# Tracing a four-layer attention network as one block, ordered by a finer engine model

## The chip, the cores and the metric

The kernel runs on one core of one Trainium2 chip. The core has five engines that matter here: PE (TensorE, the matrix engine), DVE (VectorE), ACT (ScalarE), POOL (GpSimd) and SP (SyncE, which issues the transfers). Each engine works through its own list of instructions in the order in which the build has put them, and waits on semaphores where it needs what another engine makes. The metric is the time of one execution on the device in microseconds; of several runs the median is taken.

## The reference

The reference is a network of two parts over 256 latent rows and 256 context rows of width 1024, in float32. The first part has four layers with the same frame and different mixers: attention with grouped heads and a window (layer 0), latent attention with low-rank queries and keys (layer 1), a matrix LSTM in chunks (layer 2), and grouped attention again (layer 3).

```python
layers = [window_gqa_mixer, mla_mixer, mlstm_mixer, window_gqa_mixer]   # shortened
for i in range(4):
    sh_l, sc_l, gt_l = modulation(c, w_ada, b_ada)
    sh_c, sc_c, gt_c = modulation(c_ctx, w_ada, b_ada)
    h_l = rmsnorm(x_lat, g_pre) * (1.0 + sc_l[:, None, :]) + sh_l[:, None, :]
    h_c = rmsnorm(x_ctx, g_pre) * (1.0 + sc_c) + sh_c
    y_l, y_c = mixer(h_l, h_c, need_ctx=i < 3)
    x_lat = x_lat + gt_l[:, None, :] * rmsnorm(y_l, g_post)
    if i < 3: x_ctx = x_ctx + gt_c * rmsnorm(y_c, g_post)
```

The second part works on the latent rows alone: one projection, three mixers side by side (a sparse one, one with a window, one with forget gates), a gated merge of the three, an output projection, and a feed-forward part with a convolution.

```python
h = rms_norm(x, norm_mix); cols = split_columns(h @ w_in)
o_a, o_b, o_c = nsa_mixer(cols, ...), swa_mixer(cols, ...), fox_mixer(cols, ...)
proj = einsum('btnm,nmd->btnd', stack([o_a, o_b, o_c]), w_branch)
x = x + (sigmoid(cols['merge']) * proj).sum(axis=2) @ w_out
x = x + conv_ffn(rms_norm(x, norm_ffn), w_gate, w_up, conv_w, conv_b, w_down)
```

## The kernel before

Every product of two float32 matrices is made of three matmuls on rounded halves: a value is split into a high half and the rest, and high by high, low by high and high by low are summed in one PSUM bank. In `gemm_a` these are L366, L367 and L368 (512 columns each), in `gemm_b` L378, L379 and L381 (256 columns). Weights come from DRAM in pieces of 512 KB: `load_part` has SP load a piece (L356), ACT copy its high half (L345, into wh or Q) and DVE subtract for the low one (L347, into wl or P). PSUM tiles come from three sets of banks: three named mm for products, two named S for scores, three named tp for transposes and small sums.

The two streams, c (context) and l (latent), lie in xc0, xc1, xl0 and xl1 of 128 rows each. `normed` squares them on ACT (L603) for the sum of squares and scales them on DVE (L606). `turn` transposes the result on PE (L618, four transposes into one tp bank), modulates it on ACT (L625, two for each bank) and splits it on DVE (L627 and L628, into thc and tlc or thl and tll). With that the first products of a layer can start.

At the end of a layer, `out_proj` makes four products of 24 matmuls for each stream, one for each half of the width and each 128 rows. Behind each one ACT squares the bank (L663) and DVE multiplies it by a gate (L664), after which the bank is free. `finish` does the `turn` of the stream that was finished before; it is called within `out_proj` of the other stream (L661), at the product whose number is in the constant FIN.

Attention in layers 0 and 3 (`gqa`) takes a head at a time: two matmuls and a mask make a score tile S (L908, L909, L912), DVE takes the row maxima (L913, L914), ACT the exponentials (L921), DVE scales by the row sums (L929, four for a group of four heads), PE transposes (L942), ACT and DVE copy the transposes out in turn (L736, L740), and PE multiplies them by the values (L947). Layer 1 (`mla`) has the same steps as `softmax` (L1110 to L1129) and `back` (L1142 to L1155), layer 2 (`mlstm`) its own. A filler, `ada_steps`, issues the modulation of the next layer a piece at a time (L540, eight small matmuls together) at a pace set by the table PACE.

The text of the kernel sets dependencies, not the order on the engines. All instructions are traced first. When the context closes, the framework puts those of each engine in order, with a model of how long each one takes; program order and a few marked priorities decide between those that are ready. The last lines of the kernel, where the change is, open the net's context and run it: `Net.run` first does the setup and the first `turn`, then the four layers, then the mixers and the feed-forward part.

Of the kernel before, what the change touches and what calls it, by code (L numbers as in the profile page):

```python
# [2036 lines left out]


def body(tc, A, out, upto=99):
    with ExitStack() as stack:  # L2040
        net = Net(tc, A, out, stack, upto)
        with net.inner_guard():
            net.run()
# [18 lines left out]
```

## Time and profile before

| | us |
|---|---|
| median of three runs | 1456.51 (1456.22 to 1456.57) |
| the profiled execution's own time | 1455.3 |
| its span | 1453.5 |
| PE busy | 1418.6 |
| DVE busy | 1044.2 |
| ACT busy | 736.0 |
| POOL busy | 51.5 |

The profile shows one execution. Its page gives the busy time of each engine, then the chain of work that ended last, followed back from the last instruction; the views behind it list what an engine waited for, the busy time of a stretch, and single instructions in order of time. A matmul's shown length is longer than the distance to the next one, since matmuls are pipelined: the distance between two starts is what it costs the engine. The granted clock of the execution is 0.998 of full speed in the mean.

### The profile page before, as it was taken

The numbers are of one execution on the slowest core, as the hardware profiler recorded it, in microseconds if no ns is written. First come the engines' busy times: TensorE is split into PE (matmuls) and PEld (weight loads), VectorE is DVE, ScalarE is ACT, GpSimd is POOL, SyncE is SP. The second block draws the span as 40 slices with busy tenths as digits, with TensorE's granted clock in tenths as the row PEclk, the third lists the DMA queues.
The fourth block names the chain that finished last, engine by engine and source line by source line (L and its number), as shares of the span: only waits on it lengthen the run. The fifth ranks groups of instructions, "written<-read, shape, count | busy, mean of one in ns | idle before, by whom it ended". The sixth has DMA issues, their size and how long they took to land.

```text
span 1453.5 us, 24554 instructions
## 1 busy us (share of the span) xinstructions
PE 1418.6 (98%) x9445; PEld 1172.7 (81%) x9445; DVE 1044.2 (72%) x2241; ACT 736.0 (51%) x1447; POOL 51.5 (4%) x72
## 2 busy tenths in 40 slices
PE   7999999999999999999999999999999999999998
PEld 4776778789787778887778776778878888799987
DVE  4587866653788667793765867889687877799863
ACT  3455544442556344552634544556576555465542
POOL 0000000000000000010100000000000000211200
PEclk9999999999999999999999999999999999999999
DMA  9541215345602214515252532157524534455552
GB/s 379 202 163 44 74 56 207 94 149 186 208 32 62 73 48 147 201 52 173 87 198 73 173 125 65 60 180 240 159 96 138 174 117 158 164 198 184 180 182 97
DMA packets 63555, 203.35 MB, mean 140 GB/s; under 512 B 10329, under 2 KB 14542, under 8 KB 63438
## 3 DMA queue, kind: packets, MB, share of 16 engines
q1 hardware_dynamic: 63438, 201.79, 41.2%
q8 instruction: 74, 1.21, 0.3%
q14 instruction: 43, 0.35, 0.1%
HBM read 200.65 MB, written 1.11 MB: 139 GB/s over the span
## 4 chain that ended last, share of the span: by engine, by line
PE 82%; DVE 8%; ACT 4%; issue 3%; DMA 2%; POOL 0%; SPq 0%; ACTq 0%; DVEq 0%; POOLq 0%
PE mm L366 10%; PE mm L368 10%; PE mm L367 10%; PE mm L378 8%; PE mm L381 8%; PE mm L379 8%; PE tp L947 3%; PE tp L942 3%; PE tp L540 2%; PE tp L744 2%; PE S L378 1%; PE S L379 1%; PE S L381 1%; PE S L908 1%; DVE wl L347 1%
## 5 line engine op out<-in xcount | busy, mean ns | idle before, releaser
L347 DVE TENSOR_TENSOR wl<-wr,wh 128x1024 fp32r<-128x1024 f32 (+5 forms) x168 | 196.8, 1182 | 70.8 <-ACT wh L345 68.8
L345 ACT ACTIVATE wh<-wr 128x1024 fp32r<-128x1024 f32 (+5 forms) x172 | 174.5, 1027 | 96.6 <-PE mm L379 28.0
L378 PE MATMUL mm<-thl,wh 128*128 128x256 f32 x608 | 175.6, 289 | 0.0
L381 PE MATMUL mm<-thl,wl 128*128 128x256 f32 x608 | 174.0, 287 | 0.7 <-DVE wl L347 0.7
L379 PE MATMUL mm<-tll,wh 128*128 128x256 f32 x608 | 174.2, 287 | 0.0
L366 PE MATMUL mm<-wh,thl 128*128 128x512 f32 (+3 forms) x312 | 123.2, 395 | 0.8 <-ACT thl L693 0.5
L368 PE MATMUL mm<-wh,tll 128*128 128x512 f32 (+3 forms) x312 | 122.4, 393 | 0.0
L367 PE MATMUL mm<-wl,thl 128*128 128x512 f32 (+3 forms) x312 | 122.0, 391 | 0.0
L378 PEld LDWEIGHTS mm<-thl,wh 128*128 128x128 f32 x608 | 116.3, 191 | 4.0 <-issue 3.2
L381 PEld LDWEIGHTS mm<-thl,wl 128*128 128x128 f32 x608 | 116.0, 191 | 3.0 <-issue 1.5
L379 PEld LDWEIGHTS mm<-tll,wh 128*128 128x128 f32 x608 | 116.5, 192 | 1.5 <-issue 1.2
L366 PE MATMUL mm<-wh,thc 128*128 128x512 f32 (+2 forms) x232 | 91.5, 395 | 2.1 <-DVE thc L627 1.6
L368 PE MATMUL mm<-wh,tlc 128*128 128x512 f32 (+2 forms) x240 | 92.6, 388 | 0.5 <-DVE tlc L1918 0.3
L367 PE MATMUL mm<-wl,thc 128*128 128x512 f32 (+2 forms) x232 | 90.9, 393 | 0.0
L347 DVE TENSOR_TENSOR wl<-wrd,wh 128x1024 fp32r<-128x1024 f32 x52 | 65.9, 1270 | 26.8 <-ACT wh L345 26.5
L921 ACT ACTIVATE P<-S,nm 128x512 f32<-128x512 f32 (+1 forms) x96 | 58.5, 613 | 44.6 <-DVE nm L914 40.9
L366 PEld LDWEIGHTS mm<-wh,thl 128*128 128x128 f32 x312 | 58.7, 188 | 12.5 <-issue 1.6
L368 PEld LDWEIGHTS mm<-wh,tll 128*128 128x128 f32 x312 | 58.7, 188 | 10.8 <-issue 0.6
L345 ACT ACTIVATE wh<-wrd 128x1024 fp32r<-128x1024 f32 x52 | 53.5, 1050 | 26.0 <-PE mm L367 23.0
L367 PEld LDWEIGHTS mm<-wl,thl 128*128 128x128 f32 x312 | 58.8, 188 | 9.4
L378 PE MATMUL mm<-thc,wh 128*128 128x256 f32 (+1 forms) x216 | 65.3, 302 | 0.6 <-DVE thl L752 0.6
L381 PE MATMUL mm<-thc,wl 128*128 128x256 f32 (+1 forms) x216 | 63.4, 293 | 0.0
(564 smaller groups left out, 3730.6 us busy)
## 6 DMA issues: line engine op xcount, KB each, us to landing
ar<-in_w_l_ada_dram SPq DMA_DIRECT2D x80, 512.0 KB
wr<-in_w_l_in_dram SPq DMA_DIRECT2D x48, 512.0 KB
wr<-in_w_l_out_dram SPq DMA_DIRECT2D x32, 512.0 KB
wr<-in_w_s_mg_dram SPq DMA_DIRECT2D x24, 512.0 KB
wrd<-in_w_s_down_dram SPq DMA_DIRECT2D x22, 512.0 KB
wrd<-in_w_s_gate_dram SPq DMA_DIRECT2D x20, 512.0 KB
wrd<-in_w_s_up_dram SPq DMA_DIRECT2D x20, 512.0 KB
wr<-in_w_s_br_dram SPq DMA_DIRECT2D x12, 512.0 KB
```

What stands on the lines that cost most here:

```text
L345: nc.scalar.activation(hi[:, :kc * n], raw[:, :kc * n], AF.Copy)
L347: eng.tensor_sub(lo[:, :kc * n], raw[:, :kc * n], hi[:, :kc * n].bitcast(F32))
L366: nc.tensor.matmul(ps, xh(kk), wh[:, k, n0:n0 + n], start=kk == 0, stop=False)
L367: nc.tensor.matmul(ps, xh(kk), wl[:, k, n0:n0 + n], start=False, stop=False)
L368: nc.tensor.matmul(ps, xl(kk), wh[:, k, n0:n0 + n], start=False, stop=kk == KC - 1)
L378: nc.tensor.matmul(ps, wh[:, k, n0:n0 + m], xh(kk), start=kk == 0, stop=False)
L379: nc.tensor.matmul(ps, wh[:, k, n0:n0 + m], xl(kk), start=False, stop=False)
L381: nc.tensor.matmul(ps, wl[:, k, n0:n0 + m], xh(kk), start=False, stop=kk == KC - 1)
L540: return self.nc.tensor.matmul(ps[32 * g:32 * g + 32, :], self.cs[:, k, :], r[:, g * 256:(g + 1) * 256], start=k0 == 0 and i == 0, stop=k0 ...
L921: nc.scalar.activation(p[:, :nk], ps[:, i, :], AF.Exp, scale=scale, bias=nm[:, r:r + 1], accum_out=sm[:, r:r + 1])
L942: nc.tensor.transpose(tp[:, r, :], P[r][:, j * 128:(j + 1) * 128], self.eye)
L947: nc.tensor.matmul(o[i * 64:(i + 1) * 64, kv], vv, pT[:, 2 * i:2 * i + 2, :], start=j == 0, stop=j == nj - 1)
```

## The change

`body` opens a named block around everything that it traces. The block's instructions are put in order when it closes, and its argument asks for the finer of the framework's two timing models of the engines for that. Nothing that is computed changes, nor does any tile, number of slots or constant.

```diff
 def body(tc, A, out, upto=99):
-    with ExitStack() as stack:
+    with tc.block(name="all", schedule_with_timeline_sim=True), ExitStack() as stack:
         net = Net(tc, A, out, stack, upto)
         with net.inner_guard():
             net.run()
```

Both kernels have the same instructions on each engine: 8723 matmuls and transposes on PE, 2145 on DVE, 1177 on ACT, 68 on POOL and 469 transfers on SP. Of these, 6387 on PE, 1701 on DVE, 883 on ACT, 3 on POOL and 219 on SP stand at another place in their engine's row. (The page counts more on PE, since some matmuls leave two records.) The row of the feed-forward part is nearly the same. In the rows below a name such as mm1013_5584 is a tile and the number of its buffer; the same buffer has a number higher by one in the changed kernel.

The first place is the start, on ACT: xn13 and xn14 are the squares of the context stream, Q434 and Q435 those of the latent one, and mid29 is the first modulated tile. Before:

```order
L603 ACTIVATE xn13_107,ss12_106<-xc0_75 128x1024
L446 ACTIVATE th0_89<-cc_81 128x16
L603 ACTIVATE xn14_108,ss12_106<-xc1_76 128x1024
L497 ACTIVATE mid24_168<-tp19_126 128x128
L345 ACTIVATE wh31_192<-wr30_190 128x1024
L625 ACTIVATE mid29_185<-tp28_180,bclc7_100,acolc5_98 128x256 x2
L603 ACTIVATE Q434_199,ss33_198<-xl0_77 128x1024
L603 ACTIVATE Q435_200,ss33_198<-xl1_78 128x1024
L625 ACTIVATE mid41_223<-tp40_218,bcll6_99,acoll4_97 128x256 x2
```

Now:

```order
L603 ACTIVATE xn13_108,ss12_107<-xc0_76 128x1024
L603 ACTIVATE xn14_109,ss12_107<-xc1_77 128x1024
L446 ACTIVATE th0_90<-cc_82 128x16
L497 ACTIVATE mid24_169<-tp19_127 128x128
L345 ACTIVATE wh31_193<-wr30_191 128x1024
L603 ACTIVATE Q434_200,ss33_199<-xl0_78 128x1024
L625 ACTIVATE mid29_186<-tp28_181,bclc7_101,acolc5_99 128x256 x2
L603 ACTIVATE Q435_201,ss33_199<-xl1_79 128x1024
L345 ACTIVATE wh54_294<-wr53_292 128x1024
```

The square of xl0 (Q434) moved ahead of the L625 of mid29, and the square of xc1 ahead of the small tanh (L446).

The second place is the hand-over from layer 1 to layer 2, first on PE. mm1013 and mm1014 are the last two products of the latent stream's output, tp1004 to tp1010 the transposes of the context stream. Before:

```order
L618 MATMUL tp1008_5535<-eye_83,xn993_5467 128x128
L618 MATMUL tp1008_5535<-eye_83,xn992_5466 128x128
L618 MATMUL tp1008_5535<-eye_83,xn993_5467 128x128
L366 MATMUL mm1013_5584<-Q4968_5315,thl952_5276 128x512
L367 MATMUL mm1013_5584<-P4969_5316,thl952_5276 128x512
L618 MATMUL tp1010_5545<-eye_83,xn992_5466 128x128
L618 MATMUL tp1010_5545<-eye_83,xn993_5467 128x128
L618 MATMUL tp1010_5545<-eye_83,xn992_5466 128x128
L618 MATMUL tp1010_5545<-eye_83,xn993_5467 128x128
L368 MATMUL mm1013_5584<-Q4968_5315,tll953_5277 128x512
```

Now:

```order
L618 MATMUL tp1008_5536<-eye_84,xn993_5468 128x128
L618 MATMUL tp1008_5536<-eye_84,xn992_5467 128x128
L618 MATMUL tp1008_5536<-eye_84,xn993_5468 128x128
L618 MATMUL tp1010_5546<-eye_84,xn992_5467 128x128
L618 MATMUL tp1010_5546<-eye_84,xn993_5468 128x128
L618 MATMUL tp1010_5546<-eye_84,xn992_5467 128x128
L618 MATMUL tp1010_5546<-eye_84,xn993_5468 128x128
L366 MATMUL mm1014_5612<-Q4968_5316,thl952_5277 128x512
L367 MATMUL mm1014_5612<-P4969_5317,thl952_5277 128x512
L368 MATMUL mm1014_5612<-Q4968_5316,tll953_5278 128x512
```

The 24 matmuls of mm1013 now stand in one piece ahead of the 16 transposes, and mm1014 right behind these; before, 19 matmuls of mm1013 stood behind the last transpose. On ACT at the same place, where mid1005 to mid1011 are the modulated tiles and mm1001 and mm1012 the two products ahead of mm1013, before:

```order
L625 ACTIVATE mid1005_5520<-tp1004_5515,bclc585_3187,acolc583_3185 128x256 x2
L625 ACTIVATE mid1007_5530<-tp1006_5525,bclc585_3187,acolc583_3185 128x256 x2
L625 ACTIVATE mid1009_5540<-tp1008_5535,bclc585_3187,acolc583_3185 128x256 x2
L625 ACTIVATE mid1011_5550<-tp1010_5545,bclc585_3187,acolc583_3185 128x256 x2
L663 ACTIVATE yg998_5485,ss1000_5487<-mm1001_5488 128x512
L663 ACTIVATE yg999_5486,ss1000_5487<-mm1012_5557 128x512
```

Now:

```order
L625 ACTIVATE mid1005_5521<-tp1004_5516,bclc585_3188,acolc583_3186 128x256 x2
L625 ACTIVATE mid1007_5531<-tp1006_5526,bclc585_3188,acolc583_3186 128x256 x2
L625 ACTIVATE mid1009_5541<-tp1008_5536,bclc585_3188,acolc583_3186 128x256 x2
L663 ACTIVATE yg998_5486,ss1000_5488<-mm1001_5489 128x512
L625 ACTIVATE mid1011_5551<-tp1010_5546,bclc585_3188,acolc583_3186 128x256 x2
L663 ACTIVATE yg999_5487,ss1000_5488<-mm1012_5558 128x512
```

The first L663 moved ahead of the last pair of L625 and still stands behind six L625. mm1480, mm1481 and mm1468 stand in the same way at the hand-over from layer 2 to layer 3.

The third place is the last heads of layer 3, on PE, where mm1778 is a projection of that layer and S1680, S1682, S1695 and S1697 are scores. Before:

```order
L912 MATMUL S1680_9355<-mask_469,eyeb_474 128x128
L381 MATMUL mm1778_9869<-thl1469_8351,wl1769_9802 128x256
L908 MATMUL S1682_9363<-K81498_8521,Q41662_9263 128x512
L909 MATMUL S1682_9363<-K81499_8522,Q41662_9263 128x512
L912 LDWEIGHTS eyeb_474
L912 MATMUL S1682_9363<-mask_469,eyeb_474 128x128
L378 MATMUL mm1778_9869<-thl1469_8351,wh1771_9807 128x256
L379 MATMUL mm1778_9869<-tll1470_8352,wh1771_9807 128x256
L908 MATMUL S1695_9418<-K81498_8521,Q41662_9263 128x512
L909 MATMUL S1695_9418<-K81499_8522,Q41662_9263 128x512
L912 LDWEIGHTS eyeb_474
L912 MATMUL S1695_9418<-mask_469,eyeb_474 128x128
```

Now:

```order
L912 MATMUL S1680_9356<-mask_470,eyeb_475 128x128
L908 MATMUL S1682_9364<-K81498_8522,Q41662_9264 128x512
L909 MATMUL S1682_9364<-K81499_8523,Q41662_9264 128x512
L912 LDWEIGHTS eyeb_475
L912 MATMUL S1682_9364<-mask_470,eyeb_475 128x128
L908 MATMUL S1695_9419<-K81498_8522,Q41662_9264 128x512
L909 MATMUL S1695_9419<-K81499_8523,Q41662_9264 128x512
L912 LDWEIGHTS eyeb_475
L912 MATMUL S1695_9419<-mask_470,eyeb_475 128x128
L908 MATMUL S1697_9427<-K81498_8522,Q41662_9264 128x512
L909 MATMUL S1697_9427<-K81499_8523,Q41662_9264 128x512
```

The matmuls of the projection left the spaces between the scores, where three stood within these rows and twelve between S1697 and the first transpose behind it; they stand ahead of scores of earlier heads.

## Rows read from the trace of the kernel before

**Rows 1.** The page: busy time of PE, chain by engine, the costliest DVE group

```profile
PE 1418.6 (98%) x9445; PEld 1172.7 (81%) x9445; DVE 1044.2 (72%) x2241; ACT 736.0 (51%) x1447; POOL 51.5 (4%) x72
...
PE 82%; DVE 8%; ACT 4%; issue 3%; DMA 2%; POOL 0%; SPq 0%; ACTq 0%; DVEq 0%; POOLq 0%
...
L347 DVE TENSOR_TENSOR wl<-wr,wh 128x1024 fp32r<-128x1024 f32 (+5 forms) x168 | 196.8, 1182 | 70.8 <-ACT wh L345 68.8
```

**Rows 2.** PE's waits: us in total, number of times, longest one

```profile
PE tp L494 <- DMA P<-in_w_l_mod_dram: 7.6, 2, 7.4
PE tp L744 <- DVE xl L1928: 3.1, 2, 2.0
...
PE tp L618 <- DVE xn L606: 2.3, 4, 1.3
...
PE S L908 <- ACT P L921: 1.4, 1, 1.4
PE tp L744 <- DVE P L1361: 1.3, 3, 0.7
PE S L1110 <- ACT P L1125: 1.2, 1, 1.2
PE tp L1150 <- ACT T L1145: 1.2, 2, 0.7
```

**Rows 3.** Busy time by stretch: us, PE, PEld, DVE, ACT, POOL, granted clock, DMA

```profile
24.00:278.00 254.00, 253.47 (x1842) 193.45 (x1843) 174.66 (x404) 122.50 (x270) 0.00 (x0) 1.00 0.38 134
388.00:482.00 94.00, 89.94 (x548) 73.75 (x547) 81.69 (x198) 57.64 (x133) 0.00 (x0) 1.00 0.25 84
910.00:950.00 40.00, 37.59 (x248) 26.66 (x247) 32.70 (x78) 23.72 (x54) 0.00 (x0) 1.00 0.18 61
1245.00:1262.00 17.00, 13.92 (x72) 11.41 (x71) 14.35 (x16) 9.16 (x12) 9.98 (x4) 0.96 0.37 125
```

**Rows 4.** In order of time, 14 to 18 us, ACT and PE: start, length, idle before

```profile
15.08 1.05 ACT L603 ACTIVATE Q<-xl 128x1024 f32<-128x1024 f32 x1
...
15.71 0.79 PE L366 MATMUL mm<-wh,thc 128*128 128x512 f32 x1 [1.57 <-DVE thc L627]
```

**Rows 5.** In order of time, 508 to 517 us, the hand-over to layer 2

```profile
508.35 0.40 PE L366 MATMUL mm<-Q,thl 128*128 128x512 f32 x1
...
510.50 3.75 ACT L625 ACTIVATE mid<-tp,bclc,acolc 128x256 f32<-128x256 f32 x8 [1.17 <-PE tp L618]
...
512.30 0.39 PE L366 MATMUL mm<-Q,thl 128*128 128x512 f32 x1
...
514.10 0.63 ACT L663 ACTIVATE yg<-mm 128x512 f32<-128x512 f32 x1
...
515.08 0.69 DVE L664 TENSOR_TENSOR yg<-mm,K 128x512 f32<-128x512 f32 x1
...
516.49 0.39 PE L366 MATMUL mm<-Q,thl 128*128 128x512 f32 x1
```

**Rows 6.** In order of time, 915 to 927 us, softmax and values in layer 3

```profile
915.48 0.23 PE L912 MATMUL S<-mask,eyeb 128*128 128x128 bf16 x1
...
915.75 1.42 DVE L913 TENSOR_REDUCE mx<-S 128x1 f32<-128x512 f32 x2
...
917.33 0.69 ACT L921 ACTIVATE P<-S,nm 128x512 f32<-128x512 f32 x1 [0.83 <-DVE nm L914]
...
918.16 0.50 PE L908 MATMUL S<-K,Q 128*128 128x512 f32 x1 [1.43 <-ACT P L921]
...
920.77 1.66 DVE L929 TENSOR_SCALAR P<-P,sm 128x512 f32<-128x512 f32 x4
...
924.90 1.09 PE L942 MATMUL tp<-eye,P 128*128 128x128 f32 x8
...
925.59 0.69 DVE L740 COPY T<-tp 128x512 f32<-128x512 f32 x1 [0.75 <-PE tp L942]
...
926.39 1.08 PE L947 MATMUL tp<-T,V 128*64 128x256 f32 x8
```

## Prediction

> **What bounds the kernel now.** I read the page first: the share of each engine, then the chain that ended last by engine [rows 1]. TensorE is busy 1418.6 of 1453.5 us, and 82% of the chain is its own work. So the time is TensorE's work plus the holes in it, 34.9 us. The change neither adds nor removes an instruction: the work stays, and only the holes can move. Next I read what TensorE waits for [rows 2]. 7.6 us is for the first transfer of the program, which no order can shorten. The rest is single waits of up to 2.3 us, most of them where one stage hands over to the next: there the next stage needs a value that passes PE, ACT and DVE in turn, and no other matmul is left to put between. Last I read the busy time stage by stage [rows 3]. Layer 0's attention (24 to 278 us) has TensorE busy for 253.47 of 254 us; layer 1's (388 to 482) for 89.94 of 94, with DVE at 81.69, which is 87%; the last heads of layer 3 (910 to 950) for 37.59 of 40. A better order can thus bring 27 us at the very most, while a worse one can cost far more: TensorE has no slack, and a hole of 1 us costs 1 us.
>
> **How a moved instruction is costed.** Where the orders of the two kernels differ I take durations and paces from the rows and lay them out in the new order, place by place, with pencil and paper. Three prices recur. A matmul of 512 columns costs TensorE 0.233 us (18 of them from 512.30 to 516.49 [rows 5]), a transpose 0.11 (eight L942 in 1.09, the last one's 0.2 of running out taken off [rows 6]). A score's way through the softmax of layers 0 and 3 is read from [rows 6]: from the last matmul of one score (L912, 915.48) the maximum starts 0.27 later, takes 0.68, the exponential starts 0.16 behind the maxima and takes 0.69, and the next score in that bank starts 0.14 after it. With one maximum that is 1.95 us, with two behind each other 2.65. What stands between in TensorE's order must last as long, else TensorE stands.
>
> **Part 1, the start.** ACT now squares xl0 (L603) ahead of the L625 that make the first operand of the first large matmul; before, the square came behind two of them. It takes 1.05 us, and that matmul (L366, 15.71 us) already waited 1.57 us for this chain [rows 4]. xl0 lands about when the L625 could begin, so most of the square is added: **+0.9** (0.4 to 1.3). What else moves here, another square ahead of a small tanh on ACT and a few transfers on SP's queue, hides behind the first transfer: 0.
>
> **Part 2, the hand-overs between layers.** Layer 0 to 1, at 304 us: 48 matmuls now stand where the transposes of the normed stream (L618) waited 1.3 us for DVE, the longest of the four in [rows 2]. Covered: **-1.35**. Layer 1 to 2, at 508 us [rows 5]: before, the 16 transposes stood inside the first third of the 24 matmuls of mm1013, and the other matmuls covered what ACT and DVE make of them. Now come all 24 matmuls, then all 16 transposes, then mm1014, which reuses the bank of mm1001. That bank is free only after L663 on ACT and L664 on DVE, and ACT does L663 behind six L625, which need the transposes. From 508.35 the matmuls last to 513.9; six transposes and a passing of 0.3 later it is 514.9; six L625 at 0.47 give 517.7; L664 starts 0.6 to 1.0 after L663's start, say 518.4, and takes 0.69; mm1014 starts at 519.0 instead of 516.49. **+2.5** (1.5 to 3.2). DVE's four L347 ahead of L606 cost nothing here: what they delay is now waited for later. Layer 2 to 3, at 803 to 811 us, moves in the same way with mm1480, mm1481 and mm1468: **+2.5** again. At 280 us the same rows move, but nine matmuls and an ada group stay behind the transposes: 0.
>
> A rule bears on this place. The trace before has mm1014 begin one pace after mm1013's last matmul. The Trainium skill (Perfetto Trace Analysis, Matmuls) says that independent matmul groups should rotate through PSUM banks so that the evacuation of one overlaps the matmuls of the next; the old order agrees with it. If the rotation held in the new one too, both terms would be 0 and the forecast 5 us lower.
>
> **Part 3, the last heads of layer 3.** This is the largest term. Before, the projections mm1762, mm1776 and mm1778 were spread between the scores and transposes of the last softmaxes; now they stand some 45 us of work earlier in the row, and the last four softmaxes are nearly alone, with 13 matmuls of the output projection ahead of S1680 and two later. I laid out the four from S1677 with the prices above, 0.4 for each of the four L929 and 0.69 for a copy of transposes (L740) [rows 6]. TensorE then stands 1.9 us before S1695 (a way of 2.65, and only S1682's 0.7 between), 1.5 before the first L942, and 0.9, 0.8, 0.5, 0.7, 1.0 and 1.1 at six more places: 8.4 in all. Before, the stretch held 2.4 of holes (40 less 37.59 [rows 3]), of which the 1.4 at L908 is the same wait. **+6** (2 to 10: low if the maxima follow the scores closer than laid out, high if DVE's L347 fall between).
>
> A second rule speaks against this change. The rows show 0.5 us of holes in 254 where projections and softmaxes are mixed. The Trainium skill (Perfetto Trace Analysis, Optimization Strategy) says that where the most-contended engine changes from regime to regime, interleaving the regimes may help; by it alone, each tail that the new order thins out costs, layers 0, 1 and 2 too.
>
> **Part 4, layer 1's attention.** Projections and the next head's scores are pulled ahead of the value products (`back`), so the 1.2 at L1110 and most of the 1.2 at L1150 [rows 2] are covered: -2.5 with a smaller one. At the end of the layer less is left to put between: 15.0 us of TensorE's work stands against 16 to 18 of DVE's (nine L1146, which I price as L740's 0.69, and five L347 and two L800 at 1.18 [rows 1] among them), and the last products are followed at once by the matmul that needs them: +3.5. **+1** (-2 to +6).
>
> **Part 5, smaller places.** Layer 0's last scores have 1.1 to 1.5 us between where 1.95 is needed, four times: +3. Layer 2's last transposes feed their products with 0 to 0.3 us between; the way over a copy is 1.1 (from the fourth L942 behind 924.90, at 925.25, to L947 at 926.39 [rows 6]), and it is missed three times: +2.5. In the mixers (1060 to 1245 us) three groups stand closer to the prepared weights or the turned tile that they need, at 0 to 7 us of other work instead of 3 to 9: +2 (0 to 8). The waits at L744 for L1361 and some like them get more between: -2. At the end of the mixers the two L744 that wait 3.1 in all for L1928 [rows 2] have 3.8 and 5.0 us of other work ahead instead of 1.1 and 1.3: -3. The feed-forward part, from 1262 us on, keeps its order: 0. **+2.5** (-6 to +14).
>
> **The sum.** 0.9 - 1.35 + 5.0 + 6 + 1 + 2.5 = +14.05. On the profiled execution's own 1455.3 us that is 1469.35. The median of the runs, 1456.5, lies 1.2 above that execution, within what two executions differ by; I stay with the lower base and forecast **1469 us**.
>
> **Rivals.**
> (a) The new order covers waits and opens none worth the name. For it: 304 us and the end of the mixers are plainly better. Then Part 2's -1.35, Part 4's -2.5 and Part 5's -5 stand, 1446.5 with all and 1452 with half of them, say **1449 us**. It decides if the ways between the engines are shorter than 1.95 us; against it, they are read from rows where no engine was behind. Chance 0.2.
> (b) The holes trade places: hand-overs and start +5.9 against -8.9 of (a), and tails of a few us: 1453.6 to 1459.4, **1456 us**. Chance 0.17. That the change does nothing at all is ruled out by the order: 6387 of 8723 matmuls and transposes stand elsewhere.
> (c) DVE takes over. From the point where DVE's work behind the last projection of a layer exceeds TensorE's, the tail goes at DVE's pace; layer 1, with DVE at 87% [rows 3], is there already, and layers 0 and 2 would lose as layer 3 does: 6 us for each of three more tails in place of 1, 3 and 2.5, that is 1481, and with the mixers' high end 1487: **1484 us** (1478 to 1495). Chance 0.18.
> (d) The granted clock falls in the thin tails. It was 1.00 at 910 to 950 us and 0.96 in the 17 us at 1245 to 1262 where TensorE was busy for 13.92 [rows 3]. At 0.96 over 70 us of tails that is +2.8, or 1472: inside the forecast's own range, and without a chance of its own.
>
> **How the numbers follow.** The forecast's case (1459.5 to 1478) has 0.45, so faster 0.2 from (a), same 0.17 from (b), and slower 0.63 from the forecast and (c). A change of 0.2%, 2.9 us, is about what a measurement of this kernel can tell from none. The range leaves out the fast half of (a) and the slow half of (c), 0.1 each: **1449 to 1484 us**. The forecast's own range is 1459.5 to 1478.
>
> **What would show it.** In the profile after: waits of about 2.5 us at mm1014's and mm1481's first L366 for L664; in the last 40 us of layer 3 several waits of 0.5 to 2 us at L908 for L921 and at L942 for L929; the wait for L606 of 1.3 and those for L1928 gone; the first L366 at about 16.6 us; and TensorE's busy time still 1418 us. The prediction is wrong if TensorE's holes sum to less than 40 us, or if the pace of the matmuls itself changes, which no row makes me expect.

## The result

The changed kernel takes 1531.3 us in the median (1526.6 to 1534.9) where the one before takes 1456.5 on the same chip: 1.051 times as long, with an interval from 1.0493 to 1.0528. The forecast was 1469 and the range ended at 1484: the side was right, the size was wrong by a factor of six. The profiled execution of the changed kernel took 1533.5 us, its span is 1531.7, 78.2 longer than before, and its granted clock is 0.975 in the mean, where it was 0.998.

The page after, in the lines that answer to [rows 1]:

```profile
PE 1441.8 (94%) x9445; PEld 1195.3 (78%) x9445; DVE 1033.6 (67%) x2241; ACT 733.7 (48%) x1447; POOL 56.9 (4%) x72
...
PE 80%; DVE 7%; DMA 6%; ACT 4%; issue 2%; SPq 0%; POOL 0%; ACTq 0%; DVEq 0%; POOLq 0%
...
L347 DVE TENSOR_TENSOR wl<-wr,wh 128x1024 fp32r<-128x1024 f32 (+5 forms) x168 | 196.5, 1180 | 84.9 <-ACT wh L345 75.2
```

The work is the same and one instruction of DVE costs what it cost. What grew are two things. The time in which TensorE stands went from 34.9 to 89.9 us (1531.7 less 1441.8), which is 55 us. And TensorE's busy time went from 1418.6 to 1441.8 with the same instructions, which is 23 us: some of them ran at the lower of the clock's two levels. The two figures are the profile's own split and not exact, since the ends of matmuls are modelled: in layer 1's attention the holes grew by 3.8 us and the busy time fell by 3.5, though the granted clock fell there too, from 1.00 to 0.98. So the 23 us may be less than what the clock cost.

What TensorE waits for after, in the columns of [rows 2]:

```profile
PE tp L494 <- DMA P<-in_w_l_mod_dram: 8.7, 2, 8.5
PE mm L366 <- DVE yg L664: 7.5, 5, 2.5
PE tp L1545 <- DVE P L1533: 4.9, 1, 4.9
PE mm L366 <- DVE thc L627: 4.8, 3, 3.3
PE tp L540 <- DMA ar<-in_w_l_ada_dram: 4.4, 4, 1.5
PE mm L366 <- ACT thc L799: 4.4, 3, 2.5
PE tp L942 <- DVE P L929: 3.6, 3, 1.5
PE mm L366 <- DVE mid L780: 3.4, 2, 2.2
PE S L908 <- ACT P L921: 3.1, 4, 1.7
PE mm L366 <- ACT thl L693: 2.9, 2, 1.9
```

L366, the first matmul of each group of three in the large products, waits 26.0 us itself: the five entries above, and 1.2 for L1206, 0.9 for L345, 0.5 for L792 and twice 0.2 further down. Before, its entries summed to 3.0 (1.6, 0.5, 0.5, 0.4). Two of these waits are at the hand-overs (2.53 each) and one at the start (3.31); many of the others are by matmuls that fill the spaces between softmaxes. In the new row they stand where their own operand isn't there yet. L606, L1928 and L1361, which stood near the head of the list of before, are gone from it. New is the wait for transfers of the modulation's weights (`ar`), 4.4 us where the list of before has none.

To see where the time went, the rows of TensorE are cut where both kernels have done the same matmuls. In the next two fences are four of these stages, before and then after, with the columns of [rows 3] (the stretch, its length, busy time of PE, PEld, DVE, ACT and POOL, granted clock, DMA): layer 0's attention, the output of layer 1 with the turn to layer 2, layer 3 up to the end of its attention, and the first half of the mixers. Before:

```profile
91.60:270.10 178.50, 178.22 (x1253) 134.27 (x1252) 127.18 (x306) 87.51 (x209) 0.00 (x0) 1.00 0.27 94
483.50:530.30 46.80, 46.43 (x209) 37.57 (x210) 27.77 (x62) 18.36 (x38) 0.82 (x4) 1.00 0.07 22
824.60:980.40 155.80, 152.57 (x945) 110.47 (x944) 120.49 (x267) 81.23 (x165) 0.00 (x0) 1.00 0.34 113
1017.00:1111.00 94.00, 92.89 (x710) 79.34 (x709) 71.19 (x199) 56.04 (x126) 1.85 (x2) 1.00 0.43 137
```

After:

```profile
92.90:288.90 196.00, 184.55 (x1254) 136.30 (x1252) 130.20 (x310) 88.39 (x213) 0.00 (x0) 0.97 0.26 86
503.40:556.00 52.60, 49.61 (x208) 40.14 (x209) 27.42 (x62) 18.27 (x38) 0.82 (x4) 0.93 0.03 11
858.90:1037.10 178.20, 160.58 (x946) 113.61 (x944) 121.55 (x258) 82.50 (x168) 0.00 (x0) 0.96 0.31 100
1076.40:1187.60 111.20, 100.00 (x710) 83.51 (x709) 75.68 (x209) 58.06 (x130) 1.85 (x2) 0.95 0.35 114
```

The first, third and fourth are longer by 17.5, 22.4 and 17.2 us: 57 of the 78. In each, the length less the busy time is the time TensorE stood (0.3, 3.2 and 1.1 before; 11.5, 17.6 and 11.2 after), and the rise of the busy time (6.3, 8.0 and 7.1) goes with a granted clock of 0.95 to 0.97 where it was 1.00. The two hand-overs, of which the second row is one, are longer by 5.8 and 5.4, the output of layer 3 by 3.0, the late mixers by 3.3, layer 2's tail by 2.7; the end of the mixers is shorter by 1.6, and the feed-forward part takes what it took. DVE is busy for 66 to 68% of the three large ones, where it was busy for 71 to 77%, so it has not become the bound.

### The profile page after: what moved, and what is told of

Read it like the earlier page. It is cut to its first block, busy times and chain, and to the rows that moved or that the text cites. A ratio compares the mean times of both kernels' runs of the same rounds, so it can differ in the third digit from the quotient of the medians.

```text
span 1531.7 us, 24545 instructions
## 1 busy us (share of the span) xinstructions
PE 1441.8 (94%) x9445; PEld 1195.3 (78%) x9445; DVE 1033.6 (67%) x2241; ACT 733.7 (48%) x1447; POOL 56.9 (4%) x72
## 3 DMA queue, kind: packets, MB, share of 16 engines
q8 instruction: 74, 1.21, 0.3%
## 4 chain that ended last, share of the span: by engine, by line
PE 80%; DVE 7%; DMA 6%; ACT 4%; issue 2%; SPq 0%; POOL 0%; ACTq 0%; DVEq 0%; POOLq 0%
PE mm L366 11%; PE mm L368 11%; PE mm L367 11%; PE mm L379 8%; PE mm L378 8%; PE mm L381 8%; PE tp L540 2%; PE tp L947 2%; PE tp L942 2%; PE tp L744 2%; DMA ar<-in_w_l_ada_dram 1%; PE S L379 1%; PE S L381 1%; PE S L378 1%; PE S L908 1%
## 5 line engine op out<-in xcount | busy, mean ns | idle before, releaser
L345 ACT ACTIVATE wh<-wr 128x1024 fp32r<-128x1024 f32 (+5 forms) x172 | 174.1, 1026 | 124.2 <-PE mm L367 31.4
L366 PE MATMUL mm<-wh,thl 128*128 128x512 f32 (+3 forms) x312 | 122.0, 394 | 5.7 <-ACT thl L693 2.9
L366 PE MATMUL mm<-wh,thc 128*128 128x512 f32 (+2 forms) x232 | 95.5, 414 | 13.9 <-DVE thc L627 4.8
L345 ACT ACTIVATE wh<-wrd 128x1024 fp32r<-128x1024 f32 x52 | 54.5, 1055 | 49.6 <-PE mm L367 27.7
L913 DVE TENSOR_REDUCE mx<-S 128x1 f32<-128x512 f32 (+1 forms) x80 | 54.4, 686 | 31.4 <-PE S L912 26.3
L366 PEld LDWEIGHTS mm<-wh,thl 128*128 128x128 f32 x312 | 59.5, 191 | 18.0 <-ACT thl L693 3.4
L366 PEld LDWEIGHTS mm<-wh,thc 128*128 128x128 f32 x232 | 46.0, 198 | 26.4 <-DVE thc L627 5.6
```

What stands on the lines that cost most here:

```text
L345: nc.scalar.activation(hi[:, :kc * n], raw[:, :kc * n], AF.Copy)
L366: nc.tensor.matmul(ps, xh(kk), wh[:, k, n0:n0 + n], start=kk == 0, stop=False)
L913: nc.vector.reduce_max(mx[:, r0:r0 + per], ps, axis=AX)
```

## Three holes read in order of time

Layer 0, 220 us, DVE, ACT and PE (start, length, idle before and what ended it):

```profile
220.35 0.69 DVE L740 COPY Z<-tp 128x512 f32<-128x512 f32 x1 [1.71 <-PE tp L947]
...
221.83 1.29 DVE L783 SCALAR_TENSOR_TENSOR Z<-mid,Z 128x512 f32<-128x512 f32 x2
...
223.21 1.06 ACT L799 ACTIVATE thc<-Z 128x1024 fp32r<-128x1024 f32 x1 [2.18 <-DVE Z L783]
...
224.32 0.79 PE L366 MATMUL mm<-wh,thc 128*128 128x512 f32 x1 [2.52 <-ACT thc L799]
...
225.41 0.77 PE L908 MATMUL S<-K,Q 128*128 128x512 f32 x1
```

The last values of a head leave PE at 220.3. They pass DVE twice and ACT once before the output projection can take them, 4.0 us in all, and in that time the row of PE has two scores and then the projection's L366 itself. It stands for 2.52 us. The score behind it, whose operands had long been there, takes 0.77, where one takes 0.50 elsewhere (at 220.32 in the same view): the clock is down.

Layer 3, 965 to 986 us, the last softmaxes, PE alone; this answers to [rows 6]:

```profile
965.82 0.50 PE L908 MATMUL S<-K,Q 128*128 128x512 f32 x1 [0.92 <-DVE Q L751]
968.28 0.49 PE L366 MATMUL mm<-Q,thc 128*128 128x512 f32 x1 [0.86 <-ACT Q L345]
971.01 0.68 PE L366 MATMUL mm<-wh,thc 128*128 128x512 f32 x1 [2.24 <-DVE mid L780]
978.50 0.50 PE L908 MATMUL S<-K,Q 128*128 128x512 f32 x1 [1.73 <-ACT P L921]
981.44 0.48 PE L942 MATMUL tp<-eye,P 128*128 128x128 f32 x1 [1.46 <-DVE P L929]
985.80 0.65 PE L947 MATMUL tp<-T,V 128*64 128x256 f32 x4 [1.12 <-ACT T L736]
```

The row at 965.82 is the score S1677, the one at 978.50 is S1695, the one at 981.44 the first transpose behind it. The prediction laid out 1.9 and 1.5 us for these two; they are 1.73 and 1.46. The 13 matmuls of the output projection that it took for cover ahead of S1680 begin with the rows at 968.28 and 971.01, and wait 0.86 and 2.24 themselves.

The mixers, 1140 to 1146 us, the longest hole that the new order makes:

```profile
1140.13 1.21 DVE L347 TENSOR_TENSOR wl<-wr,wh 128x1024 fp32r<-128x1024 f32 x1
...
1141.26 0.16 DVE L1515 TENSOR_SCALAR nm<-mx 128x8 f32<-128x8 f32 x1
...
1145.95 1.33 PE L1545 MATMUL tp<-eye,P 128*128 128x128 f32 x5 [4.89 <-DVE P L1533]
```

Between the last row maximum (L1511, done at 1140.2) and the small L1515 that needs it stands a weight's low half of 1.21 us, and behind them come the exponentials on ACT and the scaling on DVE. PE has nothing between its last score, done at 1141.06, and the transposes that need all of this.

## The experiments

All of them are one of the two kernels, with the row of an engine, or a stretch of it, held in the order of another. What a kernel computes is the same in all. What is not held is put in order by the build as before, around the rows that are held, and that changes it: with TensorE's whole row held, 1520 of the 2241 instructions of DVE in the trace stand elsewhere than in the changed kernel (compared in order by line, tile and shape), and 1167 elsewhere than in the one before. So a run with one row put back is not the changed kernel with one row exchanged. The rows are held by dependencies that order two instructions of one engine and put no wait on any:

```diff
+def pin(tc, shift):
...
+    for engine, parts in rows.items():
+        for part in parts:
+            for p, q in zip(part, part[1:]):
+                tc.add_manual_dep(by[q + shift], by[p + shift].name,
+                                  mybir.DependencyInfo(mybir.DependencyClass.NoSync, mybir.DependencyReason.DATA),
+                                  reason="pin")
```

`rows` is a packed constant, by engine its stretches, each a list of instruction numbers; `by` finds an instruction by its number, and `shift` is 1 in the changed kernel, whose block takes a number. In the diffs below the constant is written out: `before["PE"][521:1620]` is that stretch of TensorE's row in the kernel before, `after` the same of the changed one. TensorE's row has 8723 places; layer 0's attention is 521 to 1620, the hand-over to layer 2 ends at 3152, that to layer 3 at 4770, layer 3 is 4770 to 5616, the first half of the mixers 5824 to 6453.

Three theories stood against each other. One puts the loss into TensorE's row (A where a letter stands for it); its rival (B) puts it into the rows of DVE and ACT, whose instructions slip between those that TensorE waits for. The third (C) holds that no row alone is bad: the finer model makes the three rows for one another, and the loss belongs to all three together.

**TensorE's whole row put back.**

```diff
+ORDER = {"PE": [before["PE"][0:8723]]}
...
     with tc.block(name="all", schedule_with_timeline_sim=True), ExitStack() as stack:
         net = Net(tc, A, out, stack, upto)
         with net.inner_guard():
             net.run()
+            pin(tc, 1)
```

> Finer model for every engine, but TensorE's whole row is held in the order of the kernel before. Theory A (TensorE's row causes the loss: projections are placed early, the work that follows a softmax has nothing left to hide behind, and the lower clock follows from the holes): 1456 to 1464 us, holes of TensorE under 40 us, mean granted clock 0.995 or more. Theory B (the rows of DVE, ACT and SP cause it: weight splits ahead of the chain, transfers late): 1490 us or more, holes of 60 us or more. In between would divide the loss of 75 us between the two.

Measured: 1553.7 us, ratio 1.0657 (1.0626 to 1.0688). That is 22 us slower than the changed kernel. TensorE's waits in it, the first and the third:

```profile
PE S L908 <- ACT P L921: 10.4, 6, 4.2
...
PE tp L618 <- DVE xn L606: 6.9, 4, 2.6
```

The waits for L664 and L799 are gone, but the scores now wait 10.4 us for the softmax, and the turn waits 6.9 for L606 where it waited 2.3 in the kernel before. Beside the old row of TensorE, the rows that the finer model makes for DVE and ACT are worse than those of the changed kernel. So putting TensorE's row back does not take the loss away, but the run does not show what that row costs in the changed kernel, whose rows of DVE and ACT are others.

**TensorE's row put back in the three stages that lost most.**

```diff
+ORDER = {"PE": [before["PE"][521:1620], before["PE"][4770:5616], before["PE"][5824:6453]]}
+            pin(tc, 1)
```

> As the changed kernel, but TensorE's row is held in the old order in three stretches alone: layer 0's attention, layer 3's attention and the first third of the mixers, which are 17.4, 22.4 and 17.3 us longer in the trace of the changed kernel. Theory A: the stretches are independent and 57 us come back, 1470 to 1480 us; the low clock is gone in them. Theory B: under 20 us come back, 1512 us or more.

Measured: 1509.6 us, ratio 1.0354 (1.0324 to 1.0384). Of the 57 us of these stages 19.5 came back (they are still 11.6, 19.5 and 6.5 longer than before). That is near what was expected if the rows of DVE and ACT made the loss (under 20 us back), but here too these were ordered anew (851 of DVE's 2241 elsewhere than in the changed kernel). Layer 3 is hardly better than there; it stands at other places.

**TensorE's row put back at the two hand-overs.**

```diff
+ORDER = {"PE": [before["PE"][3004:3152], before["PE"][4642:4770]]}
+            pin(tc, 1)
```

> As the changed kernel, but TensorE's row is held in the old order at the two hand-overs alone (layer 1 to 2, layer 2 to 3), some 280 of 8723 rows. If the two waits of 2.5 us for L664 are all that they cost: 5.1 us less, and the low clock at 541 to 545 and 841 to 849 us stays. If the low clock there is caused by these waits: the two stretches of low clock go as well and the hand-overs give back 9 to 11 us, so 1518 to 1523 us against 1526 to 1535 of the changed kernel. If the low clock has another cause (the block of 16 transposes, say, is not it, since it goes too): it stays or turns up elsewhere.

Measured: 1526.9 us, ratio 1.0473 (1.0443 to 1.0503); the span is 7.3 us shorter than that of the changed kernel, 5.4 of it in the two stages. The medians differ by 4.4 us and the two intervals overlap, so the reading rests on the stages. Twenty microseconds at the first hand-over, in which mm1014 begins, at 535.62 in this kernel:

```profile
533.00:553.00 20.00, 20.00 (x92) 16.40 (x92) 12.10 (x33) 6.19 (x15) 0.82 (x4) 1.00 0.00 1
```

The wait is gone, and with it the low clock that followed it (the rows of the changed kernel at this place are in the next section). The 9 to 11 us that were expected back did not come: the transposes now wait for L606, 1.64 us at the first hand-over and 1.41 at the second, and 1.51 for L625 there, so the two stages are still 3.3 and 2.6 longer than before.

**One hole alone, in the kernel before.**

```diff
+ORDER = {"PE": [after["PE"][3004:3152]]}
...
     with ExitStack() as stack:
...
+            pin(tc, 0)
```

> The kernel before, with TensorE's row of the changed kernel at the hand-over from layer 1 to 2 alone (37 rows stand elsewhere; DVE, ACT and SP as before). One hole of 2.5 to 3.4 us before mm1014 is expected (3.4 if L663 stands behind all eight L625, as in the row of before). If the lower clock follows a hole: some 3 us of low granted clock behind it and 4.2 to 5.1 us more in all, 1461 to 1462.5 us. If the lower clock has another cause in the changed kernel: the granted clock stays 1.00 there and 2.5 to 3.4 us more, 1459 to 1460.5 us.

Measured: 1462.8 us over six runs, ratio 1.0043 (1.003 to 1.0057). The hole at the hand-over is 3.59 us here: ACT, whose row is that of before, does all eight L625 in one piece (3.76 us from 516.66) ahead of the first L663. Behind the hole the clock falls. The stage is 5.2 longer, 3.7 in holes and 1.5 by the clock:

```profile
521.98 0.50 PE L366 MATMUL mm<-Q,thl 128*128 128x512 f32 x1 [3.59 <-DVE yg L664]
```

```profile
518.00:522.00 4.00, 0.41 (x5) 0.17 (x3) 3.90 (x9) 4.00 (x12) 0.00 (x0) 1.00 0.00 0
522.00:526.00 4.00, 4.00 (x11) 3.14 (x12) 1.73 (x3) 0.16 (x2) 0.20 (x1) 0.57 0.02 6
```

One moved stretch of 148 places, with DVE, ACT and SP in the order of before, makes the wait and the fall of the clock behind it. Here TensorE's row alone makes the loss of a place.

**TensorE's new row of layer 3, in the kernel before.**

```diff
+ORDER = {"PE": [after["PE"][4770:5616]]}
+            pin(tc, 0)
```

> The kernel before with the coarser model, but TensorE's row in layer 3 is that of the changed kernel. Theory A: the 22.4 us of layer 3 appear in this stretch alone, 1474 to 1482 us, with holes at L908, L942 and L947 and a lower clock after them. Theory B: the coarser model arranges DVE and ACT around that row and most of the loss stays away, 1456 to 1465 us.

Measured: 1486.3 us, ratio 1.0194 (1.0165 to 1.0224). Layer 3 is 28.3 us longer, more than the 22.4 of the changed kernel. The coarser model made the rows of DVE and ACT anew around it: in this stage 218 of DVE's 266 instructions stand elsewhere than before, and 95 elsewhere than in the changed kernel.

**The rows of DVE and ACT put back, TensorE's made anew beside them.**

```diff
+ORDER = {"DVE": [before["DVE"]], "ACT": [before["ACT"]]}
+            pin(tc, 1)
```

> Finer model, but the rows of DVE and ACT are held in the order of the kernel before; TensorE's and SP's rows are the finer model's. Theory B (the rows of DVE and ACT cause the loss): 1456 to 1466 us. Theory C (a row is good or bad only with the rows that it was made with, and the finer model takes other moments for ready than the chip, for whichever engine it may order): a large loss stays, 1485 us or more, with TensorE's waits at other lines than in the changed kernel.

Measured: 1621.1 us, ratio 1.1129 (1.1089 to 1.1169), the slowest of all. Putting these rows back does not take the loss away either; it is 90 us slower than the changed kernel. TensorE's row is not that of the changed kernel (5139 of 9445 records elsewhere), so what the new rows of DVE and ACT cost by themselves stays open. The first two waits of TensorE:

```profile
PE S L908 <- ACT P L921: 20.9, 19, 2.4
PE mm L366 <- DVE yg L664: 9.5, 3, 3.6
```

**All three rows put back.**

```diff
+ORDER = {"PE": [before["PE"]], "DVE": [before["DVE"]], "ACT": [before["ACT"]]}
+            pin(tc, 1)
```

> Finer model, but TensorE's, DVE's and ACT's rows are all held in the order of before: only SP's transfers (84 of 471 at another place) stay the finer model's. If the transfers' order costs nothing: 1455.5 to 1459 us. If it holds a share (TensorE waits 4.4 us for ar in the changed kernel): 1460 to 1466 us.

Measured: 1462.7 us, ratio 1.0025 (0.9981 to 1.0069). Block and finer model are those of the changed kernel, SP's transfers are left to it, and of 75 us some 6 are left in the median. The interval has room for none and for 10. Three of the four runs lie at 1462.5 to 1464.5, above all nine of the kernel before (1455.5 to 1457.7), and one at 1454.9. The median lies where it was expected if the order of the transfers holds a share. One of TensorE's waits in the profiled run, which is one of the three:

```profile
PE tp L540 <- DMA ar<-in_w_l_ada_dram: 2.6, 2, 1.9
```

The kernel before has no wait for `ar`. The longer of these two ends at 67.74 us with a low clock behind it, and its stage is 3.5 longer. The end of the mixers is 3.1 longer, with 4.6 us of waits for L1928 instead of 3.1 [rows 2]. So the order of the three rows is the cause of nearly all of the loss; whether SP's order holds a few microseconds is not settled.

**All three rows of layer 3 put into the kernel before.**

```diff
+ORDER = {"PE": [after["PE"][4770:5616]], "DVE": [layer 3, 254 of DVE in after], "ACT": [layer 3, 123 of ACT in after]}
+            pin(tc, 0)
```

> The kernel before with the coarser model, but in layer 3 TensorE's, DVE's and ACT's rows are all those of the changed kernel. Theory C (rows made for each other): the 22.4 us of the changed kernel, less than the 28.2 that TensorE's row alone cost: 1478 to 1482 us. If TensorE's row sets it all: 28 again, 1485 us.

Measured: 1478.7 us, ratio 1.0151 (1.0122 to 1.0181). Layer 3, to set beside the rows of the result, and the same stage of the run in which TensorE's row alone was moved:

```profile
826.30:1004.20 177.90, 160.66 (x946) 114.32 (x944) 121.34 (x260) 81.83 (x167) 0.00 (x0) 0.96 0.30 100
```

```profile
827.30:1011.40 184.10, 163.13 (x946) 115.66 (x945) 121.42 (x264) 81.89 (x167) 0.00 (x0) 0.94 0.29 96
```

With all three rows the stage takes 177.9 us, as in the changed kernel (178.2); with TensorE's alone 184.1. Beside the same row of TensorE, the finer model's rows of DVE and ACT are 6 us better than those that the coarser one makes. That agrees with the third theory. The run also shows that the loss of layer 3 is made in layer 3 and not brought there.

**All three rows of before, in the three stages.**

```diff
+ORDER = {"PE": [before["PE"][521:1620], before["PE"][4770:5616], before["PE"][5824:6453]],
+         "DVE": [the same stages, 297, 256 and 162 of DVE in before],
+         "ACT": [the same stages, 145, 126 and 89 of ACT in before]}
+            pin(tc, 1)
```

> As the changed kernel, but in the three costly stretches (layer 0's attention, layer 3's attention, the first third of the mixers) the rows of TensorE, DVE and ACT are all held in the order of before; with TensorE's row alone held there the kernel had taken 1509.6 us. Theory C (rows made for each other): nearly all of 57 us comes back, 1471 to 1480 us. If something outside the three rows (transfers, what came before) also costs there: 1485 us or more.

Measured: 1482.4 us, ratio 1.0174 (1.0151 to 1.0197), 49 us less than the changed kernel. The three stages:

```profile
91.60:271.90 180.30, 178.44 (x1253) 134.30 (x1252) 128.96 (x307) 88.35 (x211) 0.00 (x0) 1.00 0.28 96
843.00:999.20 156.20, 152.61 (x946) 110.53 (x945) 120.62 (x266) 81.63 (x166) 0.00 (x0) 1.00 0.34 112
1036.50:1134.00 97.50, 94.42 (x710) 80.33 (x709) 74.38 (x203) 59.12 (x131) 1.83 (x2) 0.98 0.41 134
```

Clock and busy time of the first two are those of before, and their holes are 1.9 and 3.6 us (0.3 and 3.2 before). TensorE's row alone had brought back 19.5 us of the 57; all three bring back 51. That is a little more than the 1471 to 1480 us that were expected. What is left over before is the two hand-overs (5.9 and 5.2), the late mixers (5.4), and smaller places.

**The better places of the new row, in the kernel before.** Three kernels, to see whether some of the changed order is worth keeping.

```diff
+ORDER = {"PE": [after["PE"][409:521], after["PE"][1776:1880], after["PE"][3612:4191],
+                after["PE"][5710:5824], after["PE"][7251:7511]]}
+            pin(tc, 0)
```

> The kernel before, with TensorE's row of the changed kernel in the five stretches where the trace of the changed kernel was shorter (row numbers 409 to 521, 1776 to 1880, 3612 to 4191, 5710 to 5824, 7251 to 7511: by 0.4, 2.0, 0.9, 0.3 and 1.6 us). If the pieces keep their gain under the coarser model: 5 us faster, 1449 to 1453 us. If they need the rows of DVE and ACT that they were made with (theory C): no gain, 1455 to 1462 us.

Measured over ten runs: 1454.4 us, ratio 0.9981 (0.997 to 0.9993). The place at 304 us (1776 to 1880) is 1.4 shorter, layer 2's attention (3612 to 4191) 2.2, counted from behind a new wait of 1.19 at its start.

The second keeps three of these pieces and takes the front of layer 2 as TensorE's row stands in the kernel with the old rows of DVE and ACT, where that stage was 2.1 us shorter than before:

```diff
+ORDER = {"PE": [after["PE"][1776:1880], after["PE"][3612:4191], after["PE"][7251:7511],
+                that_kernel["PE"][3152:3612]]}
+            pin(tc, 0)
```

> As the kernel with the best pieces, without its two smallest ones, and with TensorE's row of layer 2's front as the finer model makes it beside the old rows of DVE and ACT; there the hole of 2.26 us before L744 had shrunk to 0.4 and the stretch was 2.1 us shorter. 1448 to 1452 us if the gains add up; 1455 or more if they don't.

Measured over six runs: 1452.5 us, ratio 0.9967 (0.9953 to 0.998): faster than both kernels, by 0.33%. The gain is at 304 us (1.45) and in layer 2's attention (3.8); the new piece at the front of layer 2 lost 2.0, with a wait of 3.05 for a transfer of `ar` in it.

The third keeps the two pieces that gained, and nothing else:

```diff
+ORDER = {"PE": [after["PE"][1776:1880], after["PE"][3612:4191]]}
+            pin(tc, 0)
```

> The kernel before with TensorE's row of the changed kernel in two places alone: the hand-over from layer 0 to layer 1 at 304 us (104 rows) and layer 2's attention (579 rows); all else in the old order. Both places were shorter than before with this row in the run of the best pieces, by 1.45 and 3.8 us, and that run's other two pieces cost 2.0 and 1.2. If the places add up and nothing behind them is disturbed: 1.0 us less than that run gains nothing elsewhere, that is before less 5.25 less 0 to 0.7 at the start, some 1451 us beside 1456.6, ratio 0.996 (0.995 to 0.9975), and the wait for L606 of 1.3 us gone. The rival: the gains were a difference between two executions, and the time is that of before within 0.1%.

Measured over twelve runs: 1455.2 us, ratio 0.9997 (0.9986 to 1.0008): no difference, so the rival of the expectation holds. The wait for L606 is down to 0.9 us in three places, and the two stages are shorter by 1.3 and 2.2, but the second piece pays for its gain at both ends. Its first moved matmul, the score L1327, now stands ahead of the products that covered its wait and waits 1.19 us for L1316 on DVE, and layer 2's tail is 0.7 longer. Layer 1's attention is 0.9 longer by a low clock, as in the kernel with one hole, where no row was moved there either. So the gain that was counted at a place was not what the place brought.

## Why the prediction was right or wrong

**Right: the bound and the side.** TensorE has no slack, and a worse order costs more than a better one can bring. The change in the time is its holes (55 us) and its pace (23).

**The step that failed.** The forecast looked for waits mainly where the layers hand over and at their last softmaxes, took any matmul that stands between two dependent ones for cover by its length alone, and put the clock at nothing. For layer 0's attention, layer 3 and the first half of the mixers it summed 3, 6 and 2 us. They measured 17.5, 22.4 and 17.2: 35.7 of the 57.1 in holes and 21.4 in busy time at a lower clock. The cover waited for its own operands, and in the mixers a softmax had none.

**Part 1, the start.** +0.9 was said, the stage is 1.2 longer. In order of time, as [rows 4]:

```profile
14.92 1.06 ACT L603 ACTIVATE Q<-xl 128x1024 f32<-128x1024 f32 x1 [0.21 <-DMA xl<-in_x_dram]
15.98 1.00 ACT L625 ACTIVATE mid<-tp,bclc,acolc 128x256 f32<-128x256 f32 x2
...
17.50 0.79 PE L366 MATMUL mm<-wh,thc 128*128 128x512 f32 x1 [3.31 <-DVE thc L627]
```

The square stands ahead of the L625 as the order said, and the first large matmul starts 1.8 us later (16.6 was said), its wait 1.74 longer. That the sum fits is in part luck: the first transfer landed 1.06 later (TensorE's first matmul at 8.46 instead of 7.40), which is not the new order's doing, since two kernels with the old rows at the start begin as late (8.58 with one hole, 8.55 with three rows put back).

**Part 2, the hand-overs.** The wait came out as worked out, and the term was less than half of what the stage costs. In order of time, as [rows 5]:

```profile
535.46 1.47 PE L618 MATMUL tp<-eye,xn 128*128 128x128 f32 x12
...
539.84 0.68 DVE L664 TENSOR_TENSOR yg<-mm,K 128x512 f32<-128x512 f32 x1
...
540.58 0.50 PE L366 MATMUL mm<-Q,thl 128*128 128x512 f32 x1 [2.53 <-DVE yg L664]
...
541.66 0.63 PE L366 MATMUL mm<-Q,thl 128*128 128x512 f32 x1
...
542.95 0.63 PE L366 MATMUL mm<-Q,thl 128*128 128x512 f32 x1
```

mm1014 waits 2.53 us for L664, at both hand-overs, where 2.5 was worked out. But from 541.66 to 542.95 three matmuls take 1.29, 0.43 each, where the same ones took 0.233 [rows 5]: TensorE is at the lower of its two levels, 1.2 instead of 2.4 GHz, until about 544. With the clock the stages cost 5.8 and 5.4. At the first, a part is brought in: the granted clock is 0.50 from 500.1 to 506.9 us, behind holes at the end of layer 1, and the stage begins at 503.4. That mm1014 would begin right behind mm1013, by the overlap that the Trainium skill's rule on rotating banks is for (Perfetto Trace Analysis, Matmuls), is not what the trace shows. The three banks rotate as before, but the one that comes next is still being emptied, since L663 stands behind six L625 on ACT: rotating alone did not bring the overlap. At 304 us the wait for L606 is gone, as said. The stage around it (270.1 to 305.5 us before) is only 0.2 shorter, since the clock is low at its start, behind a wait for L780 of 1.12. The next one, up to layer 1's attention, is 1.1 longer, with two new waits for `ar` of 1.10 and 1.14.

**Part 3, layer 3.** Said +6, measured +22.4; the largest term of the sum failed by the most. Where softmaxes were laid out, from S1680 on, the sizes came out: 1.73, 1.46, 1.12, 0.69, 0.63 and 0.45 us, 6.1 in all, where 8.4 was laid out. The step that failed is the limit of the layout, "the last four softmaxes are nearly alone, with 13 matmuls of the output projection ahead". Those 13 were counted as cover and wait 3.1 us for their own operands, and the heads before them, where the layout did not go, hold holes of 1.01, 1.01, 1.13, 0.68, 0.35 and 0.92. Two more, 0.81 and 1.86, stand near the end. Against 3.2 before that is 14.4 in all; the other 8.0 is the clock.

**Part 4, layer 1.** Said +1, measured +0.2. As said, the waits at L1110 and L1150 shrank (from 1.2 and 1.2 to 0.4 and 0.6) and the end of the layer opened (L1151 waits 2.8 where it waited 0.3). But its holes grew by 3.8 us in all, and the number fits only because the busy time fell by 3.5, which no term has: luck.

**Part 5, smaller places.** Layer 2's last transposes: +2.5 said, 2.7 measured. The end of the mixers: -3 said, -1.6. The feed-forward part: 0 and 0. Layer 0's attention: +3 said, +17.5. The mixers ahead of their end: +2 (0 to 8) said, +20.4 (17.2 and 3.3 with -0.1 between). In layer 0 the error is the one of Part 3: a wait is not found by looking for scores that have too little between them, since the filling matmuls wait too. In the mixers 4.9 of the 10.1 us of new holes is the softmax read above, whose transposes have nothing ahead of them; the forecast priced three groups of products there and not that one. L366's own waits rose from 3.0 to 26.0 us, and beside the start and the hand-overs no term of the sum has them.

**Rival (d), the clock.** It was priced at 2.8 us and given no chance, and the sentence that no row makes one expect another pace of the matmuls was wrong: [rows 3] has such a row, with 0.96 at 1245 to 1262 us. A change of pace was named as a sign of being wrong, and it came. TensorE's busy time rose by 23.2 us, 30% of the loss.

**Rivals (a) and (b).** The waits that they see covered are covered (L606, L1928, L1361), 6.7 us in [rows 2]; what the new order opens elsewhere is 55 us more than it covers. The half of (a) was summed too high: 1455.3 less half of 8.85 is 1450.9 and not 1452.

**Rival (c).** Its time was nearest of all, and its mechanism isn't there: DVE is busy for less of the span than before (67% instead of 72%), and for 66 to 68% of the three stages that lost most. The rule on interleaving that was weighed in Part 3 (the Trainium skill, Perfetto Trace Analysis, Optimization Strategy) fits the stages that lost most, since in layers 0 and 3 projections and softmaxes were mixed before; the first and third windows went from 0.3 and 3.2 us of holes to 11.5 and 17.6.

**The cause.** The order of the rows of TensorE, DVE and ACT together makes nearly all of the loss: shown by the run with all three put back (1.0025, with 1.0069 as the interval's end), and in layer 3 by the run with all three moved (+22.1 of 22.4). How the loss divides between the three rows is not shown, since a row that was not held was made anew; only at one hand-over was TensorE's row moved by itself, and there it makes the loss. SP's order, which moved too, was not tested by itself. Why the finer model puts an L366 2.5 us ahead of its operand is not settled: nothing here looked into the model.

## What to carry to other kernels

A matmul that is moved into a gap covers it only if its own operand is there; when an order is read, every instruction that is called cover needs its own chain priced, at every place that moved and not only at the tails. On an engine that is busy for 98% a hole costs more than its length, since the clock can fall behind it; here 55 us of holes came with 23 more. When a scheduler orders several engines, hold all of their rows to test an order: a row that is left free is made anew around the others, and a run with one row put back measures a third order and not the share of that row.

## What the runs showed of the hardware

Behind a hole the granted clock can fall to the lower level, and this is now shown both ways: put in, a hole of 3.59 us is followed by a granted clock of 0.57 over 4 us; taken out at the hand-over, 1.00 stands where matmuls took 0.43 us each. But it does not always fall. One wait, of four transposes for L1254, has the same length in the kernel before and in the one with one hole. Before:

```profile
569.63 0.66 PE L744 MATMUL tp<-eye,mid 128*128 128x128 f32 x4 [2.26 <-ACT mid L1254]
```

With one hole:

```profile
576.79 1.00 PE L744 MATMUL tp<-eye,mid 128*128 128x128 f32 x4 [2.26 <-ACT mid L1254]
```

Behind the same 2.26 us the four took 0.66 in one and 1.00 in the other. And it falls without a long hole: in the kernel with one hole the granted clock is 0.50 from 475 to 478 us, in layer 1's attention, where the holes just ahead are 0.27 and 0.33 us and no row was moved. Each of these is one execution of a kernel; the mean granted clock of the kernel before itself lies between 0.995 and 1.000 over its runs, so executions of one kernel may differ in this. What decides is open, and no run was made for it.
